# A norm's output turned by VectorE and DRAM instead of TensorE, ahead of the mixers of a two-layer trunk

## The chip, the core and the metric

The kernel runs on one core of a Trainium2 chip. The time is device microseconds of one execution; the median of several runs counts, and a separate execution is profiled. Engines are named as in the profile: PE is TensorE (PEld its weight loads), DVE is VectorE, ACT is ScalarE, POOL is GpSimd, SP is SyncE. PSUM is the memory that PE writes its results to, SBUF the memory that holds tiles of 128 partitions, and DRAM lies outside the core. A DMA is issued by SP, ACT or POOL and lands some microseconds later.

## What is computed

Two layers on a sequence of 256 rows of 1024 numbers. Each layer is a half-step SwiGLU feed-forward (FFN) and a norm, then three mixers that read the same normalised stream, another norm, and another FFN and norm:

```python
def hybrid_layer(x, mem_n, ...):
    h = layer_norm(DEEPNORM_ALPHA * x + 0.5 * swiglu(x, ffn1_w_gu, ffn1_w_down), ln_g[0], ln_b[0])
    (dn_q, dn_k, dn_v, dn_b, dn_a, dn_z, sw_q, sw_k, sw_v, xa_q, gates) = jnp.split(h @ w_in, split_idx, axis=-1)
    o_dn = deltanet_branch(dn_q, dn_k, dn_v, dn_b, dn_a, dn_z, ...)
    o_sw = sliding_window_attention(sw_q, sw_k, sw_v, swa_sinks)
    o_xa = memory_cross_attention(xa_q, mem_n, w_mem_kv)
    branches = jnp.stack([o_dn, o_sw, o_xa], axis=2)
    gates = jax.nn.sigmoid(gates.reshape(B_, S_, N_BRANCH, D))
    merged = jnp.sum(gates * jnp.einsum('bsnc,ncd->bsnd', branches, w_branch), axis=2)
    h = layer_norm(DEEPNORM_ALPHA * h + merged @ w_out, ln_g[1], ln_b[1])
    return layer_norm(DEEPNORM_ALPHA * h + 0.5 * swiglu(h, ffn2_w_gu, ffn2_w_down), ln_g[2], ln_b[2])
```

The change is at the first of these norms: its result h must be laid out with the 1024 channels on the partitions before `h @ w_in` can be computed. `memory_cross_attention` also needs keys and values of the 256 memory rows, `mem_n @ w_mem_kv`, which do not depend on h.

## The kernel before

All weights come as one stream (`wst`) in the order of their use. `unit` loads a piece of [128, 1024] (512 KB) by SP into a tile `raw`; `split` makes two tiles of it, `hi` by a cast on ACT (`whi`) and the remainder `lo` by a subtraction on DVE (`wlo`). Every product of two split operands is three matmuls (`mm3`): hi by hi, hi by lo, lo by hi. There are five buffers for each of whi and wlo and four for raw, so a unit's split waits until PE has used up the unit five ahead of it, and a load waits for the split four ahead.

The 256 rows are two blocks of 128 (tb 0 and 1). The residual stream lies in the tiles h0 and h1, rows on the partitions. The input of a projection lies turned in `hT`, channels on the partitions, split into hi and lo as well.

The place of the change, in each layer, is the end of the first FFN (`Ffn.rest`) and `memory_kv`:
- the down projection ends with the second row block, in two halves of 256 columns (tiles `at`), while the first block is already in the norm;
- `Post` adds the result to the residual and calls `layernorm` for each block (statistics L277 and L280, the root L284 on ACT, the scaling L291 and L296 on DVE in halves of 512 columns). After each half, `fin` turns it: for block 0 it leaves a closure that is called between the matmuls of block 1, for block 1 it turns at once;
- `to_T` turns four squares of 128 x 128 by PE transposes (L137) into one PSUM tile `sm`, and `split` casts it to hT's hi on ACT and subtracts for lo on DVE (L125);
- `memory_kv` projects the memory: the keys first (four weight units, tiles `acc<-w`), then the values (four units, tiles `acc<-whi,w`), which are copied from PSUM to `mv_` on ACT (L521). The splits of the value units are held behind the end of the norm (`behind=post.end`) in the order of their engines;
- `mixers` starts with a projection of hT in columns of 324 (tiles `acc<-whi,hT`), row block 0 before row block 1 in each unit. It writes four PSUM tiles `acc`; there are four buffers, and the last two of them are freed by the two value copies.

A scheduler orders each engine's instructions by priority; `tc.issue_after` keeps an instruction behind another one. From `mixers` on, PE's instructions keep their program order. Each engine runs its queue in order: an instruction that waits holds up all behind it.

The FFN already turns its hidden activations in another way (`Ffn.out`): DVE turns 32 x 32 squares inside a tile (L356), POOL stores the tile to DRAM in four DMAs that each take one quarter of the partitions (L362), and one DMA reads it back (L363), so that the squares come to lie on the right partitions. A channel order that differs from the natural one is made up for in the order of the weight's rows on the host.

In `inverses`, inside the mixers, POOL clears the tiles Y and X64 (L849, L850). They lie in buffers that the memory's turned rows leave, so the clears wait for PE to be done with those.

Of the kernel before, what the change touches and what calls it, by code (L numbers as in the profile page):

```python
# [17 lines left out]
P = 128  # L18
D = 1024
S = 256  # L20
# [3 lines left out]
KD = D // P  # L24
# [14 lines left out]
def tile_trunk(ctx, tc, x, xT, mem, memT_, wst, lnp, memln, cvw, rows, cst, out):  # L39
    nc = tc.nc  # L40
# [6 lines left out]
    p2 = ctx.enter_context(tc.tile_pool(name="p2", bufs=2))  # L47
# [4 lines left out]
    pd = ctx.enter_context(tc.tile_pool(name="pd", bufs=2, space=bass.MemoryType.DRAM))  # L52
# [71 lines left out]
    def split(hi, lo, src):  # L124
        return nc.scalar.copy(hi, src).ins, nc.vector.tensor_tensor(lo, src, hi.bitcast(F32), op=ALU.subtract).ins  # L125
# [183 lines left out]
    class Ffn:  # L309
        def __init__(self, before=None):  # L310
            self.units = []
            for q in range(KD // 2):
                if before:
                    before(q)
                self.units.append(unit(cuts=2 if before and q == 0 else 1, parts=2 if before and q in (1, 2) else 1))
            self.hu, self.bank, self.due = {}, {}, []
# [77 lines left out]

    class Post:

        def __init__(self, g_ap, b_ap, last=False):
            self.aps, self.last, self.hT = (g_ap, b_ap), last, None

        def early(self, bank):  # L400

# [6 lines left out]
        def __call__(self, tb, outs):  # L408
            if tb == 0:
                self.gb = gb(*self.aps)  # L410
                self.hT = None if self.last else new_hT()
            y = hres[tb]

            def put(q):
                return self.hT[0][:, q * 4:q * 4 + 4, :], self.hT[1][:, q * 4:q * 4 + 4, :]

            def src(j, c):
                nc.vector.scalar_tensor_tensor(y[:, c], outs[tb][j], 0.5 / ALPHA, y[:, c], op0=ALU.mult, op1=ALU.add)  # L418

            turns = []  # L420

            def fin(c):
                if self.last:

                    cc = slice(c * 512, (c + 1) * 512) if not tb else slice(*((0, 512), (512, 768), (768, 1024))[c])
                    (nc.scalar if c == 2 else nc.sync).dma_start(out[tb * P:(tb + 1) * P, cc], y[:, cc])
                elif tb == 0:

                    turns.append(lambda: to_T(put, tb, y, c))
                else:  # L430
                    to_T(put, tb, y, c)

            self.end = layernorm(y, *self.gb, 1, src, fin, [o.shape[-1] for o in outs[tb]], (512, 256, 256) if self.last and tb else (512, 512))
            return turns

    def begin(nxt, hT):
# [72 lines left out]
            return {8: lambda: again(0), 12: lambda: once(0), 14: lambda: again(1), 18: lambda: once(1)}  # L509
        return {4: vecs, 6: lambda: sums(0), 8: rows_, 11: halves_, 12: lambda: quarter(0), 14: lambda: quarter(1), 16: lambda: quarter(2), 18: lambda: quarter(3)}  # L510

    def memory_kv(mT, behind):
        mx = (lambda k: mT[k // 4][:, k % 4, :], lambda k: mT[2 + k // 4][:, k % 4, :])
        mkT = (T(pu, [P, 4, S], "u10", F32R), T(pu, [P, 4, S], "u7", F32R))
        for i, b in enumerate(projB(mx, 4, 2)):
            split(*(t[:, 2 * i:2 * i + 2, :] for t in mkT), b)
        mv_ = T(pu, [P, 2, 512], "u11")
        outs = [[acc()] for _ in range(2)]
        projA(mx, 512, 2, KD, outs, behind=behind, held=range(4))
        for tb in range(2):  # L520
            nc.scalar.copy(mv_[:, tb, :], outs[tb][0])  # L521
        return mkT, mv_

    def mixers(l, hT, mkT, mv_, post):
        xt = acc_of(hT)
        pinned[0] = True

# [128 lines left out]
        t = col("spt")  # L656
# [164 lines left out]
        def inverses():  # L821
# [21 lines left out]
            for j in range(15):  # L843
# [2 lines left out]
                nc.gpsimd.tensor_tensor(y16[:, :, j + 1:16], y16[:, :, j + 1:16], pr16[:, :, 0:n], op=ALU.add)  # L846
            nc.gpsimd.tensor_tensor(Y32.rearrange("p c h (d i) -> p (c h) d i", d=2), y16.unsqueeze(2).to_broadcast([P, 8, 2, 16]),
                                    cs[:, C_BD:C_BD + 32].rearrange("p (d i) -> p d i", d=2).unsqueeze(1).to_broadcast([P, 8, 2, 16]), op=ALU.mult)
            nc.gpsimd.memset(Y, 0.0)  # L849
            nc.gpsimd.memset(X64[qd[0], :, :, 32:64], 0.0)  # L850

        W = T(pu, [P, 1024], "w0")
        X64, X32, Y32 = (W[:, a:b].rearrange("p (c h i) -> p c h i", c=2, h=4) for a, b in ((0, 512), (512, 768), (768, 1024)))
# [277 lines left out]
    for l in range(NL):  # L1131
        mT = []
        mid = memory_T(mT, l)
        if l == 0:

            mid[2] = lambda: load(cs, cst)
            more = {4: lambda *a: xres(0), 6: lambda *a: xres(1), 8: lambda *a: small()}
        post = Post(lnp[l, 0, 0], lnp[l, 0, 1])
        f1.rest(hT, 4, [((pu, "u0"), (pu, "u1")), ((pu, "u2"), (pu, "u3"))], post, mid, ends, {} if l else more)
        kv = memory_kv(mT, post.end)  # L1140
        if l == 0:
            nc.scalar.activation(nea, rw[:, :, 8:12], AF.Exp)
            nc.vector.tensor_scalar(nea, nea, -1.0, None, ALU.mult)
        post2 = Post(lnp[l, 1, 0], lnp[l, 1, 1])
        mixers(l, post.hT, *kv, post2)
        f2 = Ffn()
        begin(f2, post2.hT)
        last = l == NL - 1
        post = Post(lnp[l, 2, 0], lnp[l, 2, 1], last)
        f2.rest(post2.hT, 6, [((pu, a), (pu, b)) for a, b in (("u0", "u1"), ("u2", "u3"), ("u4", "u5"), ("u6", "u13"))], post, behind=post2.end)  # L1150
        ends = post.end
        if not last:
            f1, hT = Ffn(), post.hT
            begin(f1, hT)
# [9 lines left out]
def _stream(i):  # L1164
    parts = []
    for l in range(NL):
# [6 lines left out]
        mk = i["w_mem_kv"][l]  # L1173
        parts.append(_kcols(mk[:, :512], 2))
        parts.append(_kcols(mk[:, 512:], 2))
        w = i["w_in"][l]
        parts.append(_kcols(np.concatenate([w[:, 1536:2056], w[:, 2696:2824]], 1), 1))
        for s in (512, 0, 1024, 2824):
            parts.extend(_kcols(w[:, c:c + 256], 4) for c in (s, s + 256))
# [62 lines left out]
```

## Time and profile before

| what | value |
|---|---|
| median of 3 runs | 1271.19 us (1271.11 to 1272.05) |
| the profiled execution: its time, its span | 1271.84 us, 1270.1 us |
| granted PE clock over the span | 0.999 |
| busy time of PE, DVE, ACT, POOL | 1258.1, 871.3, 661.5, 221.0 us |
| moved over the span | 263.56 MB, 208 GB/s |
| the norm's turn in layer 0: first and last group of transposes start | 186.64 and 195.03 us |
| the mixers' first projection starts (layer 0, layer 1) | 211.43 and 839.93 us |

A row of a timeline gives the start and the length in us, the engine, the line, the operation, output and inputs and the count; in brackets the idle time before it and what ended it. Neighbouring instructions on PE overlap, so PE's stream is read by the starts. In a row that groups instructions, behind the bar stand the busy time in us, the mean of one in ns, and the idle time before. For DMAs the last number is the median time in us from issue to landing.

### The profile page before, as it was taken

How to read it: one execution, taken by the hardware profiler on the slowest of the kernel's cores; microseconds unless marked ns; L12 is line 12 of the kernel's file. 1: busy time of each engine (PE TensorE's matmuls, PEld its weight loads, DVE VectorE, ACT ScalarE, POOL GpSimd, SP SyncE). 2: the span in 40 equal slices, each digit the busy share in tenths (PEclk: the TensorE clock that was granted, in tenths of full speed). 3: DMA queues.
4: the chain of work that ended last, by engine and by line, in shares of the span. 5: the costliest groups of instructions: out<-in, count | busy, mean ns of one | idle time of the engine just before them, and what ended most of it. 6: DMA issues, size and time to landing. Idle time of an engine off the chain costs nothing.

```text
span 1270.1 us, 18774 instructions
## 1 busy us (share of the span) xinstructions
PE 1258.1 (99%) x6916; PEld 1070.9 (84%) x6916; DVE 871.3 (69%) x1284; ACT 661.5 (52%) x982; POOL 221.0 (17%) x395
## 2 busy tenths in 40 slices
PE   9999999999999999999999999999999999999997
PEld 7888889999878888888888888899987788888886
DVE  6678576886667776665666665759776588766565
ACT  6456444655664544454454554455646654454441
POOL 1233000002331102221012220000023401122100
PEclk9999999999999999999999999999999999999999
DMA  8988765655554648787668887566554456578771
GB/s 293 322 265 286 249 210 160 205 179 137 164 151 150 240 139 258 243 242 220 215 208 246 256 255 216 178 185 212 162 158 133 134 189 226 174 248 243 240 231 74
DMA packets 78795, 263.56 MB, mean 208 GB/s; under 512 B 12528, under 2 KB 13968, under 8 KB 78704
## 3 DMA queue, kind: packets, MB, share of 16 engines
q1 hardware_dynamic: 66320, 232.40, 56.5%
q0 software_dynamic: 12240, 29.84, 8.7%
q8 instruction: 54, 0.88, 0.3%
q14 instruction: 37, 0.30, 0.1%
q10 hardware_dynamic: 144, 0.13, 0.0%
HBM read 247.48 MB, written 14.85 MB: 207 GB/s over the span
## 4 chain that ended last, share of the span: by engine, by line
PE 94%; DVE 3%; DMA 2%; ACT 1%; issue 1%; SPq 0%; DVEq 0%; ACTq 0%
PE acc L134 83%; PE at L134 3%; PE sm L134 3%; DMA raw<-in_wst_dram 2%; PE sm L137 1%; DVE wlo L125 1%; PE acc L335 1%; PE acc L332 1%; PE at L137 1%; PE acc L333 1%; ACT whi L125 1%; DVE h L291 0%; DVE h L296 0%; DVE h L418 0%; DVE bnst L277 0%
## 5 line engine op out<-in xcount | busy, mean ns | idle before, releaser
L125 DVE TENSOR_TENSOR wlo<-raw,whi 128x1024 fp32r<-128x1024 f32 (+2 forms) x405 | 487.1, 1210 | 277.0 <-ACT whi L125 275.0
L125 ACT CAST whi<-raw 128x1024 fp32r<-128x1024 f32 (+2 forms) x405 | 413.7, 1029 | 403.5 <-PE acc L134 314.8
L134 PE MATMUL acc<-whi,hT 128*128 128x512 f32 (+1 forms) x1824 | 563.1, 386 | 0.0
L134 PEld LDWEIGHTS acc<-whi,hT 128*128 128x128 f32 x1824 | 340.5, 188 | 68.9 <-issue 1.6
L134 PE MATMUL acc<-wlo,hT 128*128 128x512 f32 (+1 forms) x912 | 350.5, 384 | 0.1
L134 PE MATMUL acc<-whi,u 128*128 128x512 f32 x812 | 259.6, 392 | 0.0
L134 PEld LDWEIGHTS acc<-wlo,hT 128*128 128x128 f32 x912 | 171.6, 188 | 33.4 <-DVE wlo L125 0.9
L134 PEld LDWEIGHTS acc<-whi,u 128*128 128x128 f32 x812 | 152.3, 188 | 32.0 <-DVE u L125 0.5
L134 PE MATMUL acc<-wlo,u 128*128 128x512 f32 x406 | 158.2, 390 | 0.0
L362 POOL DMA_DIRECT2D tr<-t x176 | 96.0, 552 | 306.4 <-DVE t L356 299.4
L134 PE MATMUL acc<-hT,whi 128*128 128x256 f32 x672 | 121.8, 284 | 0.0
L134 PEld LDWEIGHTS acc<-hT,whi 128*128 128x128 f32 x672 | 104.7, 192 | 0.0
L134 PE MATMUL acc<-hT,wlo 128*128 128x256 f32 x336 | 95.1, 283 | 0.0
L134 PEld LDWEIGHTS acc<-wlo,u 128*128 128x128 f32 x406 | 76.3, 188 | 15.5
L134 PEld LDWEIGHTS acc<-hT,wlo 128*128 128x128 f32 x336 | 64.4, 192 | 0.0
L363 POOL DMA_DIRECT2D pt<-tr x44 | 25.0, 568 | 197.3 <-DMA tr<-t 151.6
L353 ACT ACTIVATE t<-acc 128x256 f32<-128x256 f32 x88 | 33.3, 379 | 37.1 <-PE acc L134 36.9
L134 PE MATMUL acc<-u,u 128*128 128x512 f32 x186 | 46.4, 394 | 0.0
L354 DVE TENSOR_TENSOR t<-t,acc 128x256 f32<-128x256 f32 x88 | 36.6, 417 | 8.1 <-ACT t L353 3.9
L134 PEld LDWEIGHTS acc<-u,u 128*128 128x128 f32 x186 | 34.6, 188 | 7.5
L553 DVE SCALAR_TENSOR_TENSOR t<-acc,cw,t 128x255 f32<-128x255 f32 (+2 forms) x72 | 34.5, 479 | 1.1
L125 DVE TENSOR_TENSOR u<-pt,u 128x512 fp32r<-128x512 f32 x44 | 28.9, 657 | 8.1 <-ACT u L125 8.1
(245 smaller groups left out, 1165.0 us busy)
## 6 DMA issues: line engine op xcount, KB each, us to landing
raw<-in_wst_dram SPq DMA_DIRECT2D x409, 512.0 KB, 4.4
tr<-t POOLq DMA_DIRECT2D x176, 64.0 KB, 3.9
pt<-tr POOLq DMA_DIRECT2D x44, 256.0 KB, 5.1
raw<-in_wst_dram SPq DMA_DIRECT2D x16, 324.0 KB, 3.0
gB<-in_lnp_dram SPq DMA_DIRECT2D x6, 512.0 KB, 6.7
bB<-in_lnp_dram SPq DMA_DIRECT2D x6, 512.0 KB, 7.0
w<-dr POOLq DMA_DIRECT2D x4, 512.0 KB, 12.6
t<-in_xT_dram SPq DMA_DIRECT2D x4, 256.0 KB, 5.4
```

The source lines that it names most:

```text
L125: return nc.scalar.copy(hi, src).ins, nc.vector.tensor_tensor(lo, src, hi.bitcast(F32), op=ALU.subtract).ins
L134: return pe(nc.tensor.matmul(*a, **k))
L137: return pe(nc.tensor.transpose(*a))
L332: nc.tensor.matmul(ps, hT[0][:, k, ts], hi[:, c], start=k == 0, stop=False)
L333: nc.tensor.matmul(ps, hT[0][:, k, ts], lo[:, c], start=False, stop=False)
L335: nc.tensor.matmul(ps, hT[1][:, k, ts], hi[:, c], start=False, stop=k == KD - 1)
L353: act = nc.scalar.activation(t[:, :, tb, :], g, AF.Silu).ins
L354: ins = nc.vector.tensor_tensor(t[:, :, tb, :], t[:, :, tb, :], u, op=ALU.mult).ins
L362: nc.gpsimd.dma_start(d[:, :, q].rearrange("b c x -> c b x"), z[32 * q:32 * q + 32].rearrange("c (b x) -> c b x", b=4))
L363: back = nc.gpsimd.dma_start(y, d.rearrange("b c q x -> (b c) (q x)")).ins
L553: nc.vector.scalar_tensor_tensor(yc[:, j, d:], b[:, j, :S - d], w[:, t:t + 1], yc[:, j, d:], op0=ALU.mult, op1=ALU.add)
```

## The change

The norm ahead of the mixers (and only this one of the three in a layer) is turned without PE. `fin` calls `leave` for each half: DVE turns its 32 x 32 squares into a tile z ("pp", L406 of the changed kernel). After a block's second half POOL stores z to a DRAM tile "tn" in four DMAs of 128 KB, in runs of 1 KB (L410). Behind the last store of block 1 POOL issues four reads, two for each block, of 256 KB in runs of 512 B (L417), into tiles "pt". `land` splits what has come back into hT: for block 0 behind the split of the keys in `memory_kv`, for block 1 ahead of the value copies. What the value units' splits are held behind is now the last DVE transpose. The two clears on POOL are held behind the last read. The rows of w_in are reordered on the host to match the new channel order. 16 PE transposes per layer, their four casts and four subtractions from PSUM go.

```diff
--- before.py
+++ after.py
@@ -394,8 +394,33 @@
 
     class Post:
 
-        def __init__(self, g_ap, b_ap, last=False):
+        def __init__(self, g_ap, b_ap, last=False, bounce=False):
             self.aps, self.last, self.hT = (g_ap, b_ap), last, None
+            self.bounce, self.backs = bounce, {}
+
+        def leave(self, tb, y, c):
+
+            if not c:
+                self.z = T(p2, [P, D], "pp")
+            cc = slice(c * 512, (c + 1) * 512)
+            ins = nc.vector.transpose(self.z[:, cc], y[:, cc]).ins
+            if c:
+                d = T(pd, [4, 32, 4, S], "tn")
+                for q in range(4):
+                    out_ = nc.gpsimd.dma_start(d[:, :, q].rearrange("b c x -> c b x"), self.z[32 * q:32 * q + 32].rearrange("c (b x) -> c b x", b=4)).ins
+                self.backs[tb] = d
+            if tb and c:
+                with tc.issue_after(out_):
+                    for t, d in self.backs.items():
+                        back = self.backs[t] = T(p2, [P, 2, 512], "pt")
+                        for i in range(2):
+                            self.read = nc.gpsimd.dma_start(back[:, i].rearrange("p (q x) -> p q x", q=4), d[:, :, :, i * P:i * P + P].rearrange("b c q x -> (b c) q x")).ins
+            return ins
+
+        def land(self, tb, c):
+            ts = slice(tb * P, (tb + 1) * P)
+            hi, lo = (self.hT[n][:, c * 4:c * 4 + 4, ts].rearrange("p k (q s) -> p q k s", q=4) for n in range(2))
+            return split(hi, lo, self.backs[tb][:, c].rearrange("p (q k s) -> p q k s", q=4, k=4))
 
         def early(self, bank):
 
@@ -424,6 +449,8 @@
 
                     cc = slice(c * 512, (c + 1) * 512) if not tb else slice(*((0, 512), (512, 768), (768, 1024))[c])
                     (nc.scalar if c == 2 else nc.sync).dma_start(out[tb * P:(tb + 1) * P, cc], y[:, cc])
+                elif self.bounce:
+                    self.left = self.leave(tb, y, c)
                 elif tb == 0:
 
                     turns.append(lambda: to_T(put, tb, y, c))
@@ -431,6 +458,8 @@
                     to_T(put, tb, y, c)
 
             self.end = layernorm(y, *self.gb, 1, src, fin, [o.shape[-1] for o in outs[tb]], (512, 256, 256) if self.last and tb else (512, 512))
+            if self.bounce:
+                self.end = self.left
             return turns
 
     def begin(nxt, hT):
@@ -509,19 +538,25 @@
             return {8: lambda: again(0), 12: lambda: once(0), 14: lambda: again(1), 18: lambda: once(1)}
         return {4: vecs, 6: lambda: sums(0), 8: rows_, 11: halves_, 12: lambda: quarter(0), 14: lambda: quarter(1), 16: lambda: quarter(2), 18: lambda: quarter(3)}
 
-    def memory_kv(mT, behind):
+    def memory_kv(mT, post):
+        behind = post.end
         mx = (lambda k: mT[k // 4][:, k % 4, :], lambda k: mT[2 + k // 4][:, k % 4, :])
         mkT = (T(pu, [P, 4, S], "u10", F32R), T(pu, [P, 4, S], "u7", F32R))
         for i, b in enumerate(projB(mx, 4, 2)):
-            split(*(t[:, 2 * i:2 * i + 2, :] for t in mkT), b)
+            ends = split(*(t[:, 2 * i:2 * i + 2, :] for t in mkT), b)
+        with tc.issue_after(ends[0]), tc.issue_after(ends[1]):
+            for c in range(2):
+                post.land(0, c)
         mv_ = T(pu, [P, 2, 512], "u11")
         outs = [[acc()] for _ in range(2)]
         projA(mx, 512, 2, KD, outs, behind=behind, held=range(4))
+        for c in range(2):
+            post.land(1, c)
         for tb in range(2):
             nc.scalar.copy(mv_[:, tb, :], outs[tb][0])
         return mkT, mv_
 
-    def mixers(l, hT, mkT, mv_, post):
+    def mixers(l, hT, mkT, mv_, post0, post):
         xt = acc_of(hT)
         pinned[0] = True
 
@@ -846,8 +881,9 @@
                 nc.gpsimd.tensor_tensor(y16[:, :, j + 1:16], y16[:, :, j + 1:16], pr16[:, :, 0:n], op=ALU.add)
             nc.gpsimd.tensor_tensor(Y32.rearrange("p c h (d i) -> p (c h) d i", d=2), y16.unsqueeze(2).to_broadcast([P, 8, 2, 16]),
                                     cs[:, C_BD:C_BD + 32].rearrange("p (d i) -> p d i", d=2).unsqueeze(1).to_broadcast([P, 8, 2, 16]), op=ALU.mult)
-            nc.gpsimd.memset(Y, 0.0)
-            nc.gpsimd.memset(X64[qd[0], :, :, 32:64], 0.0)
+            with tc.issue_after(post0.read):
+                nc.gpsimd.memset(Y, 0.0)
+                nc.gpsimd.memset(X64[qd[0], :, :, 32:64], 0.0)
 
         W = T(pu, [P, 1024], "w0")
         X64, X32, Y32 = (W[:, a:b].rearrange("p (c h i) -> p c h i", c=2, h=4) for a, b in ((0, 512), (512, 768), (768, 1024)))
@@ -1135,14 +1171,14 @@
 
             mid[2] = lambda: load(cs, cst)
             more = {4: lambda *a: xres(0), 6: lambda *a: xres(1), 8: lambda *a: small()}
-        post = Post(lnp[l, 0, 0], lnp[l, 0, 1])
+        post = Post(lnp[l, 0, 0], lnp[l, 0, 1], bounce=True)
         f1.rest(hT, 4, [((pu, "u0"), (pu, "u1")), ((pu, "u2"), (pu, "u3"))], post, mid, ends, {} if l else more)
-        kv = memory_kv(mT, post.end)
+        kv = memory_kv(mT, post)
         if l == 0:
             nc.scalar.activation(nea, rw[:, :, 8:12], AF.Exp)
             nc.vector.tensor_scalar(nea, nea, -1.0, None, ALU.mult)
         post2 = Post(lnp[l, 1, 0], lnp[l, 1, 1])
-        mixers(l, post.hT, *kv, post2)
+        mixers(l, post.hT, *kv, post, post2)
         f2 = Ffn()
         begin(f2, post2.hT)
         last = l == NL - 1
@@ -1173,7 +1209,7 @@
         mk = i["w_mem_kv"][l]
         parts.append(_kcols(mk[:, :512], 2))
         parts.append(_kcols(mk[:, 512:], 2))
-        w = i["w_in"][l]
+        w = i["w_in"][l].reshape(4, KD, 32, -1).transpose(1, 0, 2, 3).reshape(D, -1)
         parts.append(_kcols(np.concatenate([w[:, 1536:2056], w[:, 2696:2824]], 1), 1))
         for s in (512, 0, 1024, 2824):
             parts.extend(_kcols(w[:, c:c + 256], 4) for c in (s, s + 256))
```

DVE, layer 0, from the scaling of row block 0 (h0) to the aggregate of row block 1's statistics; wlo is the weight remainder of the last key unit, sm the turned squares in PSUM, at the end of the down projection. Before:

```order
L296 SCALAR_TENSOR_TENSOR h0_221<-h0_221,rstd_313_1610,bB_309_1599 128x512 x2
L418 SCALAR_TENSOR_TENSOR h1_222<-at_237_1211,h1_222 128x256
L125 TENSOR_TENSOR wlo_338_1802<-raw_336_1800,whi_337_1801 128x1024
L277 BN_STATS bnst_317_1671<-h1_222 128x6
L125 TENSOR_TENSOR hT_310_1602<-sm_315_1645,hT_310_1602 128x4x128
L125 TENSOR_TENSOR hT_310_1602<-sm_316_1664,hT_310_1602 128x4x128
L418 SCALAR_TENSOR_TENSOR h1_222<-at_238_1212,h1_222 128x256
L277 BN_STATS bnst_317_1671<-h1_222 128x6
L280 BN_AGGR bnmv_318_1679<-bnst_317_1671 128x2
```

Now:

```order
L296 SCALAR_TENSOR_TENSOR h0_221<-h0_221,rstd_313_1610,bB_309_1599 128x512 x2
L406 STREAM_TRANSPOSE pp_315_1620<-h0_221 128x512
L125 TENSOR_TENSOR wlo_340_1796<-raw_338_1794,whi_339_1795 128x1024
L406 STREAM_TRANSPOSE pp_315_1620<-h0_221 128x512
L443 SCALAR_TENSOR_TENSOR h1_222<-at_237_1211,h1_222 128x256
L443 SCALAR_TENSOR_TENSOR h1_222<-at_238_1212,h1_222 128x256
L277 BN_STATS bnst_317_1665<-h1_222 128x6 x2
L280 BN_AGGR bnmv_318_1673<-bnst_317_1665 128x2
```

Further on in the same queue of the changed kernel, from the scaling of row block 1 (h1) to the remainders of the four value units:

```order
L296 SCALAR_TENSOR_TENSOR h1_222<-h1_222,rstd_319_1675,bB_309_1599 128x512 x2
L406 STREAM_TRANSPOSE pp_321_1685<-h1_222 128x512 x2
L125 TENSOR_TENSOR wlo_346_1837<-raw_344_1835,whi_345_1836 128x1024
L125 TENSOR_TENSOR wlo_349_1855<-raw_347_1853,whi_348_1854 128x1024
L125 TENSOR_TENSOR wlo_352_1873<-raw_350_1871,whi_351_1872 128x1024
L125 TENSOR_TENSOR wlo_355_1891<-raw_353_1889,whi_354_1890 128x1024
```

Two transposes now stand where two subtractions from sm stood, and two more stand between the norm's end and the first value unit's wlo.

ACT, layer 0, from the split of the second half of the keys (u10) to the second value copy (u11 is mv_); whi of 128x648 are the first units of the mixers. Before:

```order
L125 CAST u10_323_1706<-acc_326_1709 128x512
L125 CAST whi_362_1936<-raw_361_1935 128x648
L125 CAST whi_365_1954<-raw_364_1953 128x648
L125 CAST whi_368_1972<-raw_367_1971 128x648
L521 COPY u11_339_1834<-acc_340_1835 128x512
L125 CAST whi_371_1990<-raw_370_1989 128x648
L521 COPY u11_339_1834<-acc_341_1836 128x512
```

Now:

```order
L125 CAST u10_325_1700<-acc_328_1703 128x512
L125 CAST whi_361_1920<-raw_360_1919 128x648
L125 CAST whi_364_1938<-raw_363_1937 128x648
L125 CAST whi_367_1956<-raw_366_1955 128x648
L125 CAST hT_310_1602<-pt_323_1694 128x4x4x32 x2
L125 CAST whi_370_1974<-raw_369_1973 128x648
L125 CAST hT_310_1602<-pt_324_1697 128x4x4x32 x2
L556 COPY u11_341_1832<-acc_342_1833 128x512
L125 CAST whi_373_1992<-raw_372_1991 128x648
L556 COPY u11_341_1832<-acc_343_1834 128x512
```

The casts of what has come back (hT<-pt, row block 0 and then 1) moved in front of the value copies.

POOL, layer 0, from the FFN's last read to the second clear, as it is now (before, the clears followed the first row directly):

```order
L363 DMA pt_231_1200<-tr_232_1201 128x512
L410 DMA tn_316_1624<-pp_315_1620 32x4x256 x4
L410 DMA tn_322_1689<-pp_321_1685 32x4x256 x4
L417 DMA pt_323_1694<-tn_316_1624 128x4x128 x2
L417 DMA pt_324_1697<-tn_322_1689 128x4x128 x2
L886 MEMSET w0_468_2586 32x8x32
L885 MEMSET w1_469_2587 128x1024
```

Eight stores and four reads moved in between, the reads of both blocks behind the stores of both.

## The prediction

> **What bounds the kernel now.** I read the page first (span, busy time, the chain that ended last), then the timeline of PE around the transposes, then the timelines of DVE, ACT and POOL at the same place. From the page:
>
> ```profile
> span 1270.1 us, 18774 instructions
> PE 1258.1 (99%) x6916; PEld 1070.9 (84%) x6916; DVE 871.3 (69%) x1284; ACT 661.5 (52%) x982; POOL 221.0 (17%) x395
> PE acc L134 83%; PE at L134 3%; PE sm L134 3%; DMA raw<-in_wst_dram 2%; PE sm L137 1%; DVE wlo L125 1%; PE acc L335 1%; PE acc L332 1%; PE at L137 1%; PE acc L333 1%; ACT whi L125 1%; DVE h L291 0%; DVE h L296 0%; DVE h L418 0%; DVE bnst L277 0%
> ```
>
> PE is the bound: busy 99%, and the chain is nearly all matmuls, with the transposes (L137) standing in it. So whatever leaves PE's stream shortens the span by its place in that stream, as long as nothing arrives late in its stead. The place itself, layer 0, in PE's timeline (start, length, instruction):
>
> ```profile
> 186.47 0.28 PE L134 MATMUL at<-whi,u 128*128 128x256 f32 x1
> 186.64 0.66 PE L137 MATMUL sm<-cs,h 128*128 128x128 f32 x4
> 187.05 0.36 PE L134 MATMUL acc<-w,whi 128*128 128x256 f32 x1
> 187.30 0.66 PE L137 MATMUL sm<-cs,h 128*128 128x128 f32 x4
> ...
> 187.91 0.28 PE L134 MATMUL acc<-w,wlo 128*128 128x256 f32 x1
> ...
> 193.72 0.40 PE L134 MATMUL acc<-w,whi 128*128 128x256 f32 x2
> ...
> 194.08 0.28 PE L134 MATMUL acc<-w,whi 128*128 128x256 f32 x1
> 194.32 0.63 PE L137 MATMUL sm<-cs,h 128*128 128x128 f32 x4
> 195.41 0.36 PE L134 MATMUL acc<-w,wlo 128*128 128x256 f32 x1
> ```
>
> **The change part by part: PE.** Sixteen transposes per layer leave the stream, four groups of four. Lengths overlap, so I count starts. Undisturbed, three matmuls of 256 columns take 0.36 us (193.72 to 194.08), 0.12 each. From 186.47 to 187.91 stand three such matmuls, 0.36 us, but 1.44 pass: the first two groups cost 1.08. From 194.08 to 195.41 stand two, 0.24 us, but 1.33 pass: the other two cost 1.09. Together 2.17 us in layer 0. Layer 1 shows the same place:
>
> ```profile
> 814.97 0.28 PE L134 MATMUL at<-whi,u 128*128 128x256 f32 x1
> 816.41 0.28 PE L134 MATMUL acc<-w,wlo 128*128 128x256 f32 x1
> ...
> 822.58 0.28 PE L134 MATMUL acc<-w,whi 128*128 128x256 f32 x1
> 823.91 0.36 PE L134 MATMUL acc<-w,wlo 128*128 128x256 f32 x1
> ```
>
> Again 1.44 and 1.33, so 2.17. Two layers: **4.34 us** off PE, if nothing takes their place. The order of PE's other rows is unchanged, and so is SP's.
>
> A mean duration would mislead here:
>
> ```profile
> L137 PE MATMUL sm<-cs,h 128*128 128x128 f32 x80 | 12.4, 279 | 0.5 <-DVE h L296 0.4
> ```
>
> Thirty-two times 0.279 us would be 8.9 us, but the next matmul starts 0.41 us after the first of four transposes (186.64 to 187.05), so a transpose takes a tenth of a microsecond of the stream. The Trainium skill ("TensorE: Matmul & The Clock Gate", Part 4: PE-mode transpose) gives about 275 ns for one in a kernel's context; as an estimate from that page 32 of them are 8.8 us and the sum would be 1263.0. The row's duration agrees with it, the spacing of the starts does not, and the spacing decides.
>
> **DVE.** What must come in time is read on the clock of before, with PE 2.17 us ahead of it behind the transposes.
>
> ```profile
> 185.85 1.40 DVE L296 SCALAR_TENSOR_TENSOR h<-h,rstd,bB 128x512 f32<-128x512 f32 x2
> 191.14 0.26 DVE L280 BATCH_NORM_AGGREGATE bnmv<-bnst 128x2 f32<-128x24 f32 x1
> 193.47 1.41 DVE L296 SCALAR_TENSOR_TENSOR h<-h,rstd,bB 128x512 f32<-128x512 f32 x2
> 194.80 3.49 DVE L125 TENSOR_TENSOR wlo<-raw,whi 128x1024 fp32r<-128x1024 f32 x3
> ...
> L356 DVE STREAM_TRANSPOSE t<-t 128x512 f32<-128x512 f32 x44 | 31.3, 711 | 1.3
> L277 DVE BATCH_NORM_STATS2 bnst<-h 128x6 f32<-128x256 f32 x24 | 9.8, 424 | 0.5
> L418 DVE SCALAR_TENSOR_TENSOR h<-at,h 128x256 f32<-128x256 f32 x12 | 5.0, 415 | 2.4 <-PE at L134 2.4
> ...
> 200.23 0.39 PE L134 MATMUL acc<-whi,w 128*128 128x512 f32 x1
> 211.43 0.31 PE L134 MATMUL acc<-whi,hT 128*128 128x324 f32 x1
> ```
>
> The first block's norm ends at 187.25. Up to the aggregate of the second block DVE now runs two transposes of 0.71, one weight remainder of 1.16 (3.49 for three), two L418 of 0.42 and two statistics of 0.42, and no longer the two hT remainders: 187.25 + 4.26 = 191.5, against 191.14. The rest of the norm is as long as before (191.14 to 194.88), so it ends at 195.25, its two transposes at 196.7. Behind them in DVE's queue stands the remainder of the first value unit, done at 197.9. PE starts on the values at 200.23 - 2.17 = 198.06 and needs that remainder with its second matmul. That fits by 0.2 us or more (the lengths are added whole, though instructions overlap a little); I cost it at nothing. Without that cover each microsecond of delay costs one per layer.
>
> **POOL and the DMAs.** Not shown by the trace of before: a store in runs of 1 KB (128 KB each) and a read in runs of 512 B (256 KB each). The nearest rows are the FFN's turning and that of the values among the mixers, on the same queue:
>
> ```profile
> 132.26 2.19 POOL L362 DMA_DIRECT2D tr<-t  x4 [5.25 <-DVE t L356]
> 138.40 0.57 POOL L363 DMA_DIRECT2D pt<-tr  x1 [3.94 <-DMA tr<-t]
> ...
> 355.93 4.44 POOL L605 DMA_DIRECT2D tv<-t  x8
> 364.04 0.56 POOL L610 DMA_DIRECT2D u<-tv  x1 [1.18 <-DMA tv<-t]
> ...
> pt<-tr POOLq DMA_DIRECT2D x44, 256.0 KB, 5.1
> w<-dr POOLq DMA_DIRECT2D x4, 512.0 KB, 12.6
> u<-tv POOLq DMA_DIRECT2D x4, 256.0 KB, 3.2
> ...
> 130.00:143.00 13.00, 13.00 (x59) 10.75 (x58) 8.01 (x9) 7.34 (x9) 2.76 (x5) 1.00 0.91 307
> 355.00:367.00 12.00, 12.00 (x121) 9.64 (x121) 6.32 (x9) 11.13 (x30) 6.39 (x13) 1.00 0.82 235
> 197.00:211.00 14.00, 14.00 (x76) 11.89 (x75) 8.06 (x11) 5.64 (x8) 0.30 (x1) 1.00 0.56 166
> ```
>
> The second block's four stores are issued from 196.8 on (0.1 for the handover) at 0.55 each (2.19 for four); the last starts at 198.5. A last store was waited for until 4.5 us after its issue in the FFN (133.9 to 138.4) and 4.2 in the mixers (359.8 to 364.0): landed at 202.7. Then come this block's two reads; those of the first block went out before them. A read lands after 3.2 us (values) to 5.1 us (FFN), so the second block's first half is back between 205.9 and 207.8. The last three rows are stretches (share of the DMA engines busy and GB/s at the end): the new transfers run where the DMA engines are busy 0.56, below both neighbours, so I take the values' 3.2 and **205.9**, and leave the rest to the shorter runs.
>
> **ACT, where a late read would show.** The two casts of the second block now stand ahead of both value copies (L521), and PE's last two banks of the first projection are those that the copies set free.
>
> ```profile
> 210.23 0.59 ACT L521 COPY u<-acc 128x512 f32<-128x512 f32 x1 [0.67 <-PE acc L134]
> 211.63 0.73 ACT L125 CAST whi<-raw 128x648 fp32r<-128x648 f32 x1 [0.81 <-PE acc L134]
> 212.27 0.58 ACT L521 COPY u<-acc 128x512 f32<-128x512 f32 x1
> ```
>
> The first projection now starts at 211.43 - 2.17 = 209.26. The weight cast between the two copies waits for PE and can't start before 209.46 (211.63 - 2.17). Ahead of it ACT needs the two casts, of the copies' size and so some 0.6 each, and a copy of 0.59: a first half that is back by **207.7** delays nothing. With 205.9 there is 1.8 us to spare; every microsecond past 207.7 is one lost per layer. The clears on POOL stand behind the reads, and their first reader is the inversion inside the mixers, a later stage: nothing. The new row order of w_in is made on the host.
>
> **The sum.** Off PE 4.34, added to the path nothing: the profiled execution took 1271.84 us (span 1270.1 and 1.7 around it), so 1267.5. It lies 0.65 above the median of the runs, so I predict 1271.2 - 4.3 = **1266.9**, a gain of 0.34%.
>
> **The rivals.**
> 1. *The read is late and eats part of the gain.* With the FFN's 4.5 and 5.1 the half is back at 198.5 + 9.6 = 208.1, 0.4 past the limit: 0.8 us lost, 1267.7. At the gain's end it would be 2.17 past, 1271.2. For it: runs of 512 B and stores of twice the size, unseen here. Against: the freer DMA engines. 17%.
> 2. *The read is so late that the kernel gets slower.* Place: ACT's wait for the second block's read, with the value copies behind it. It decides from 207.7 + 2.17 = 209.9, that is from 7.2 us for the read after stores landed at 202.7. The one slow read of this queue (w<-dr, 12.6) would bring 215.3: 7.6 lost per layer, 15.2 - 4.3 = 10.9 slower, 1282.1. Against: it is 512 KB, broadcast, in pairs. 5%.
> 3. *DVE holds up POOL's issues.* If each issue waited for the DVE instruction in progress (1.16), four stores and a read would be 5.8 us later, the half back at 211.7, 4.0 past the limit: 8.0 - 4.3 slower, 1274.9. Against it stands the spread of one issue over all 176 stores, beside a DVE that is busy 69%:
>
> ```profile
> L362 POOL DMA_DIRECT2D tr<-t x176: 548/550/709, 21.4 to 1210.3; - x176
> ```
>
> The Trainium skill ("SBUF — State Buffer", SBUF: two separate sides) warns that GpSimd can't write descriptors while VectorE runs in a two-port mode, 620 ns becoming some 3100; the estimate from that page, 2.5 us more for each of five issues, would be 1271.2 - 4.3 + 2 x 10.7 = 1288.3. The row, at most 709, disagrees for the instructions that run here. 2%.
> 4. *The held value weights are late on DVE.* If DVE's norm is 1 us longer than counted, 0.8 per layer is lost: 1268.5. 5%.
> 5. *Transposes cost PE their whole record*: 1271.2 - 8.9 = 1262.3. 1%.
> 6. *The gain goes back later*, since PE waits for weights that it reaches 2.17 us sooner: 1271.2. Against: PE is busy 99% behind this place. 3%.
>
> **How the numbers follow.** My forecast, no new wait, has 67% with its own range 1266.0 to 1268.0 (the runs spread by 0.9). About 0.2%, 2.5 us, is what a measurement of this kernel can tell from no change; faster by more ends at 1268.7. Faster: 67 + 1 + 4 of the fourth + 10 of the first = 82%. Within: 7 of the first, 1, 3 and 1 of the second = 12%. Slower: 6%. Range 1265.9 to 1270.5: it takes in the forecast, the fourth and most of the first (its 0.8 and up to 1.8 us of waiting per layer), and leaves out some 15%.
>
> **What would show it.** PE: no sm<-cs,h rows at these two places, "acc<-w" at the spacing of 0.12, and the first hT matmul 2.17 us nearer to the last "at" matmul. POOL: stores of 0.55, the second block's reads issued about 4.2 us after its last store, landing in 3 to 5. ACT: no idle time put down to the second block's read, the second copy directly behind its weight cast. I am wrong if PE idles before an hT matmul, or before the first value matmul that needs wlo.

## The result and the profile after

The change made the kernel slower: 1273.96 us median (22 runs, 1271.10 to 1278.81) against 1271.32 before on the same chip (22 runs, 1269.87 to 1276.62), a ratio of **1.0023 (95% interval 1.0016 to 1.0030)**. The forecast was 1266.9, the range 1265.9 to 1270.5. The profiled execution of the changed kernel took 1272.81 us. From its page:

```profile
span 1270.9 us, 18754 instructions
PE 1254.2 (99%) x6884; PEld 1067.2 (84%) x6884; DVE 874.7 (69%) x1292; ACT 661.4 (52%) x982; POOL 235.9 (19%) x419
L134 PE MATMUL acc<-whi,hT 128*128 128x512 f32 (+1 forms) x1824 | 563.4, 386 | 3.8 <-ACT u L556 3.8
```

PE runs 32 instructions fewer and is busy 3.9 us less, and yet the span is 0.8 longer. The last row holds the new thing: 3.8 us in which matmuls waited for the value copies (L556; L521 before), where the same row of before has no idle time. Set one by one beside their partners of before (the 32 transposes left out), the matmuls of this execution start earlier or later by the following steps (negative is earlier):

| place | layer 0 | layer 1 |
|---|---|---|
| the norm's turn | -2.2 | -2.2 |
| the mixers' first projection | +0.9 | +3.35 |
| the second norm | +1.1 | +0.9 |
| elsewhere | within 0.3 | -0.9 near 970 us |

So the saving came as counted, and layer 1's first projection alone gave back more than that layer had saved. POOL's timeline of the changed kernel, both layers (start, length, what, and in brackets the idle time before it and what ended it):

```profile
196.14 2.18 POOL L410 DMA_DIRECT2D tn<-pp  x4 [4.10 <-DVE pp L406]
198.31 1.51 POOL L417 DMA_DIRECT2D pt<-tn  x2
202.80 1.49 POOL L417 DMA_DIRECT2D pt<-tn  x2 [2.97 <-ACT whi L125]
...
824.42 1.09 POOL L410 DMA_DIRECT2D tn<-pp  x2 [4.11 <-DVE pp L406]
827.89 1.09 POOL L410 DMA_DIRECT2D tn<-pp  x2 [2.37 <-issue]
828.98 1.52 POOL L417 DMA_DIRECT2D pt<-tn  x2
833.25 1.49 POOL L417 DMA_DIRECT2D pt<-tn  x2 [2.75 <-ACT whi L125]
```

In layer 0 block 1's reads start at 202.80, as predicted (202.7). (The releaser named there is the last by the profile, but ACT has nothing to do with a store; what the reads wait for is the stores' landing.) In layer 1 a pause of 2.37 us stands between the second and the third store, with "issue" as its cause: POOL waits for nothing that the profile shows. How long the reads take, over all eight (a group's issue time in ns, then issue to landing in us):

```profile
L417 POOL DMA_DIRECT2D pt<-tn x8: 749/752/768, 198.3 to 834.0; - x8
DMA to landing us min/median/max: 5.0/6.0/6.7
```

The prediction took 3.2. ACT, in layer 0 and in layer 1, at the casts of block 1 and the value copies behind them:

```profile
209.25 0.62 ACT L125 CAST hT<-pt 128x512 fp32r<-128x512 f32 x1 [0.27 <-DMA pt<-tn]
209.78 0.58 ACT L556 COPY u<-acc 128x512 f32<-128x512 f32 x1
...
839.22 0.62 ACT L125 CAST hT<-pt 128x512 fp32r<-128x512 f32 x1 [2.16 <-DMA pt<-tn]
840.00 0.62 ACT L125 CAST hT<-pt 128x512 fp32r<-128x512 f32 x1 [0.17 <-DMA pt<-tn]
840.53 0.58 ACT L556 COPY u<-acc 128x512 f32<-128x512 f32 x1
```

And PE, at the same place of layer 1:

```profile
838.12 0.31 PE L134 MATMUL acc<-whi,hT 128*128 128x324 f32 x1
841.16 0.42 PE L134 MATMUL acc<-whi,hT 128*128 128x324 f32 x1 [2.73 <-ACT u L556]
...
842.28 0.42 PE L134 MATMUL acc<-whi,hT 128*128 128x324 f32 x1 [0.41 <-ACT u L556]
```

This is the place that the second rival named: the read lands, the casts run, the copies behind them free the two PSUM banks late. Some of the wait belongs to the order on ACT and not to the read: the first cast of block 1 ended at 839.84, PE went on at 841.16 behind the first copy and stood another 0.41 us for the second. No run puts the copies ahead of the casts, so how the wait divides between the two isn't shown. Why the read is late is in the DMA engines' share (next to last column; GB/s last), in the stretch where block 1's stores and all reads travel. Before:

```profile
200.00:208.00 8.00, 8.00 (x38) 6.49 (x37) 4.23 (x7) 3.00 (x5) 0.30 (x1) 1.00 0.54 160
828.00:836.00 8.00, 8.00 (x40) 6.58 (x39) 4.56 (x7) 3.27 (x5) 0.30 (x1) 1.00 0.64 188
```

After:

```profile
200.00:208.00 8.00, 8.00 (x36) 6.44 (x35) 4.41 (x7) 3.42 (x6) 1.81 (x3) 1.00 1.03 353
828.00:836.00 8.00, 8.00 (x36) 6.40 (x35) 4.74 (x7) 3.02 (x5) 4.31 (x7) 1.00 1.01 336
```

The engines are full for eight microseconds. Half of the stores and all reads, 1.5 MB, over 8 us are some 190 GB/s; on top of the 160 that ran there before, that is about the 353. The total fits better than its parts: of the packets that started from 200 to 208 us, those of POOL's queue make 160 GB/s and the weight loads 192; from 828 to 836 us they make 98 and 238, so the weight loads themselves moved more there than before.

### The profile page after: what moved, and what is told of

The parts are those of the page before. It is cut to its first block, busy times and chain, and to the rows that moved or that the text cites. A ratio compares the mean times of both kernels' runs of the same rounds, so it can differ in the third digit from the quotient of the medians.

```text
span 1270.9 us, 18754 instructions
## 1 busy us (share of the span) xinstructions
PE 1254.2 (99%) x6884; PEld 1067.2 (84%) x6884; DVE 874.7 (69%) x1292; ACT 661.4 (52%) x982; POOL 235.9 (19%) x419
## 4 chain that ended last, share of the span: by engine, by line
PE 88%; DMA 4%; DVE 3%; issue 2%; POOL 2%; ACT 1%; DVEq 0%; POOLq 0%; ACTq 0%
PE acc L134 79%; PE at L134 3%; PE sm L134 3%; DMA raw<-in_wst_dram 2%; DVE wlo L125 2%; DMA w<-dr 1%; PE sm L137 1%; PE acc L335 1%; PE acc L332 1%; PE acc L333 1%; ACT whi L125 1%; PE at L137 1%; POOL t L880 1%; DMA pt<-tn 0%; POOL l L871 0%
## 5 line engine op out<-in xcount | busy, mean ns | idle before, releaser
L1074 POOL TENSOR_TENSOR u<-u,gt 128x512 f32<-128x512 f32 x16 | 20.8, 1298 | 78.2 <-DVE gt L1072 74.2
```

The lines of the kernel that those rows point to most:

```text
L1074: nc.gpsimd.tensor_tensor(mg[tb][:, js], mg[tb][:, js], gt[tb][:, js], op=ALU.add)
```

## The experiments

Each is the changed kernel with one edit, unless said otherwise. Times are medians; ratios are to the kernel before (1272.36 us for the first four, 1272.06 for the next four, 1271.92 in one execution for the last three), measured on the same chip.

**Without the trip, and with the trip unread.** In the first, stores and reads are left out; in the second they run, but nobody reads what comes back. Both split the tile z in place of the tile that came back, so the channels don't lie where the weights expect them, and all other work stays (without the trip, the two clears wait for the last transpose):

```diff
-            return split(hi, lo, self.backs[tb][:, c].rearrange("p (q k s) -> p q k s", q=4, k=4))
+            return split(hi, lo, self.zs[tb][:, c * 512:(c + 1) * 512].rearrange("p (q k s) -> p q k s", q=4, k=4))
```

> Leaves out the stores and the reads: hT is split straight from the tile that DVE's transposes wrote, so channel blocks don't come to their partitions; all other work stays, the transposes on PE gone. Theory A (the second block's reads land about 6 us after their issue, the value copies stand behind their casts on ACT, and PE waits for both) and theory B (the new transfers slow the weight loads): the 4.34 us off PE stay whole in both, 1271.3 - 4.3 = 1267.0, ratio 0.9966, no wait before an hT matmul beyond the 0.25 us of before. Theory C (taking the transposes out of PE's stream does not shorten it, or DVE's two longer places cost it): 1270 or more.

> Keeps all stores and reads of the changed kernel, but splits hT from the transposed tile, as in the run without the trip; so the transfers run and nobody waits for what they bring. A alone: as without the trip, 1267.0. B: ACT still waits for raw units of the mixers (2.93, 1.66 and 1.30 us before the first three in layer 0 of the changed kernel), and PE for the copies behind them; 0.5 to 1.5 us per layer stay lost, 1268 to 1270.

Without the trip 1267.89 us, ratio 0.9967 (0.9954 to 0.9979); with the trip unread 1268.02, ratio 0.9970 (0.9957 to 0.9983). So the 4.3 us of transposes are real, and some 4 MB of extra traffic costs nothing as long as nothing waits for it: the weights have room. The loss is that the read is waited for, and what follows from that wait.

**Longer runs.** Each read takes two quarters of the features, in runs of 2 KB instead of 512 B, and needs only the stores of its two quarters (`land` takes its half out of both reads):

```diff
-self.read = nc.gpsimd.dma_start(back[:, i].rearrange("p (q x) -> p q x", q=4), d[:, :, :, i * P:i * P + P].rearrange("b c q x -> (b c) q x")).ins
+self.read = nc.gpsimd.dma_start(back[:, i], d[:, :, 2 * i:2 * i + 2].rearrange("b c q x -> (b c) (q x)")).ins
...
```

> The same reads, number and bytes, but cut by quarters of partitions and not by halves of channels: runs of 2 KB in place of 512 B. If the short runs make the reads slow (A1): issue 0.57 in place of 0.75, landing 3.2 to 5 in place of 6.0, the second block back 1.5 to 3 us sooner, 1268 to 1270.5. If the load on the DMA engines does (A2): landing stays at 5.5 to 6.5 and the time at 1273 to 1274.

1270.03 us, ratio 0.9987 (0.9977 to 0.9997). The issue fell from 0.75 to 0.56 us, but the reads still landed after 6.1 (5.4 to 6.7): short runs were not what made them slow. So the landing came out as the second theory (A2) had it, the time as the first (A1). By the trace, the gain came from earlier issues (200.5 and 202.5 in layer 0) and because the pause of 2.37 us no longer stood among layer 1's stores.

**More of block 0 first.** Three weight units of the projection run on block 0 before block 1 is needed, instead of one:

```diff
-        projA(xt, MOD, 1, KD, outs, 3)
+        projA(xt, MOD, 1, KD, outs, 3, (), 3)
```

> The first projection of the mixers takes three weight units with row block 0 before row block 1 has its first turn (three times 0.885 us of work where there was one), so PE first needs the second block and the value copies 1.77 us later. A and B: up to 1.77 us per layer come back, 1270 to 1271.5. If PE's wait lay elsewhere (C): 1274.

1270.04 us, ratio 0.9983 (0.9971 to 0.9996). PE still waited 1.6 us for the value copies in layer 1.

**Both together.**

> The changed kernel with two edits together: the reads cut by quarters of the features, so that each run of data is 2 KB, and three weight units of the mixers' projection on block 0 ahead of block 1's (two before). If what is lost is only that the two halves of the trip come too late for TensorE, the two add up: the first alone left 1.1 us of TensorE's waits at the projection, and a third unit of block 0's products is worth about 2 us there, so no wait of TensorE above 0.5 us in either layer and a time of 1267.6 to 1269.0 us, ratio to before 0.9965 to 0.9980. If something else holds part of the loss (the transfers' load on the weights, a later give-back), it stays at 0.998 to 0.999, where each edit alone was.

**1267.60 us, ratio 0.9964 (0.9950 to 0.9977): faster than both kernels**, and level with the kernel that makes no trip at all. (Its expectation counts two units of block 0 ahead in the changed kernel; there is one.) PE's three longest waits by releaser (total, times, longest):

```profile
PE sm L1154 <- DVE pp L1151: 1.5, 1, 1.5
PE acc L134 <- ACT whi L125: 0.9, 1, 0.9
PE sm L137 <- DVE h L296: 0.6, 2, 0.4
```

The 1.5 us at the kernel's start stand in the kernel before as well. The value copies (L556) are gone from the list, although the reads land no sooner (6.5 median). The wait of 0.9 lies at 9.6 us, in the first FFN; at the mixers' projection PE is busy throughout in both layers.

**Is it the load, or what such a read costs?** Three runs. First, block 0's reads directly behind block 0's stores:

```diff
+                with tc.issue_after(self.read) if tb else nullcontext():
...
-            if tb and c:
                 with tc.issue_after(out_):
-                    for t, d in self.backs.items():
+                    for t, d in ((tb, d),):
```

> The changed kernel, but block 0's two reads stand right behind block 0's four stores on GpSimd's queue, ahead of block 1's stores. They are then issued near 195 to 197 us in layer 0, where the transfer engines' share was 0.04 to 0.33, and block 1's reads have their stretch with half a megabyte less in it. Theory 'load' (a read lands late because stores, reads and weight loads fill the engines from 200 to 208 us): block 0's reads land in 2.5 to 4.5 us after issue, block 1's in 4 to 5.5. Rival 'a read costs that' (512 runs of 512 bytes each from the software queue need 6 us whatever else moves): all land in 5.5 to 6.5. The time hangs on block 1's stores, which leave some 1.3 us later, against a shorter landing: 1271.5 to 1274.

The first one, issued at 195.55 before the engines fill, landed after 3.5 us; the one behind it, at 196.3, after 5.7. The window holds the first of them alone:

```profile
L416 POOL DMA_DIRECT2D pt<-tn x1: 766/766/766, 195.5 to 195.5; - x1
DMA to landing us min/median/max: 3.5/3.5/3.5
```

The later ones took 4.2 to 5.8, so neither theory got its band whole. Block 1's stores left 0.9 us later and took longer to land, and the time was 1274.20, just past the expected range, ratio 1.0014 (1.0002 to 1.0025). Second, the reads on ACT's queue (`nc.scalar` for `nc.gpsimd`):

> The changed kernel with its reads issued by ScalarE's own queue instead of GpSimd's; the stores stay on GpSimd's. ScalarE waits in its order for the stores, so its casts move. Theory 'load': the reads still land in 4.5 to 6.5 us, as they share the same full engines. Rival 'the software queue is slow': they land in about 3 us, like the read of 256 KB that took 3.2 us before. GpSimd's queue has 2048 runs fewer in each layer, so that by the count of runs (below, the moved pause) the pause of 2.4 us falls elsewhere. Time between 1268 and 1274 us: it hangs on where ScalarE is held.

From a queue that POOL has no part in the reads took 3.9 to 8.0 us, 5.4 at the median. None landed in the 3 us of the rival (3.9 at the least): the queue is not the cause. ACT itself was held longer: PE waited 3.6 us in one piece in each layer, 1277.24 us, ratio 1.0040 (1.0027 to 1.0052), over the range that was expected. Third, the weight loads of the mixers held until the trip is over:

```diff
+        seen = T(pd, [P, 2], "seen")
+        mark.append(nc.sync.dma_start(seen, post0.backs[1][:, 1, 0:2]).ins)
         projA(xt, MOD, 1, KD, outs, 3)
...
+                with tc.issue_after(mark[0]) if mark else nullcontext():
                     nc.sync.dma_start(raw[:, c], src[:, c])
```

> The changed kernel with one small store on the hardware queue that the weight loads use: it waits for block 1's last read, and the mixers' weight loads stand behind it in that queue. So the trip has the transfer engines to itself, and the mixers start some 8 to 12 us later in each layer, for want of weights: 1285 to 1305 us, which says nothing of the change. What counts is from issue to landing of the reads of 256 KB. Theory 'load': they land in 2.5 to 4.5 us (3.5 was the earliest-issued one's time with block 0's reads ahead, 3.2 that of the kernel's other read of the same size). Rival 'a read of 512-byte runs costs that': 5.5 to 6.5 us as before.

One execution, 1281.56 us, less than the 1285 that was expected at least. Its reads, all eight:

```profile
L418 POOL DMA_DIRECT2D pt<-tn x8: 747/752/766, 198.3 to 837.0; - x8
...
DMA to landing us min/median/max: 3.4/3.5/3.6
```

The same transfer from the same queue takes 3.5 instead of 6.0 once the weight loads are out of its way, and the stores land sooner too: block 1's reads could start at 201.22 instead of 202.80. **Load it is**: the weight loads and the trip together. Whether a read waits for the bytes ahead of it or for the number of transfers, no run separates.

**The pause of 2.37 us.** The kernel before has such pauses too, where they do no harm (POOL's timeline):

```profile
546.59 2.18 POOL L362 DMA_DIRECT2D tr<-t  x4 [6.75 <-issue]
...
1116.73 0.57 POOL L363 DMA_DIRECT2D pt<-tr  x1 [7.11 <-issue]
```

They come after a like count of runs on POOL's queue. So 16 small stores were added in an idle stretch ahead of layer 1:

```diff
+        if not l:
+            pad = T(pd, [16, P, 1], "pad", bufs=1)
+            with tc.issue_after(f2.last[2]):
+                for n in range(16):
+                    nc.gpsimd.dma_start(pad[n], zero)
```

> The changed kernel with 16 extra stores of one number from each of 128 partitions on GpSimd's queue, in layer 0's last idle stretch (near 586 to 595 us), where nothing waits for them. Theory 'count': GpSimd pauses 2.2 to 7 us whenever its queue has issued some 13,500 to 14,800 runs (counting 128 a transfer, 512 for the reads with runs of 512 bytes: 14,720 and 13,312 in the kernel before, 14,848 and 13,568 in the changed one). The 16 stores then bring the second pause forward by 16 transfers, from between layer 1's stores at 827.9 us to the product's stores near 747 us, where the kernel before has such a pause without loss; layer 1's reads leave 2.4 us earlier and the loss at layer 1's mixers falls from 3.35 us to about 1, the time to 1271.0 to 1272.3 us (2 to 2.5 us under the changed kernel). Rival 'place' (the pause comes from the stores themselves or from load at that place): the pause stays at layer 1's third store, and the time at that of the changed kernel.

The pause moved, the time did not follow: 1285.35 us, ratio 1.0103 (1.0089 to 1.0118). POOL's timeline of it:

```profile
764.96 2.18 POOL L362 DMA_DIRECT2D tr<-t  x4 [6.47 <-DVE w L125]
...
839.12 2.17 POOL L410 DMA_DIRECT2D tn<-pp  x4 [4.11 <-DVE pp L406]
841.28 1.51 POOL L417 DMA_DIRECT2D pt<-tn  x2
```

Layer 1's four stores now leave in one piece. The stores at 764.96, which are the sixteenth transfer before the third of those stores, leave 2.9 us after their data is there (DVE's last transpose ends at 762.09); in the changed kernel the same ones left 0.3 after. (The row names w, a tile that the same stores did not wait for in the changed kernel.) So the pause goes by count, not by place. PE's wait at layer 1's projection fell from 3.1 to 1.7. By the matmuls' starts layer 1 lost 2.0 us there instead of 3.35. But the 16 stores of 512 bytes cost some 15 us by themselves at the FFN's end. DMA share and GB/s while they ran:

```profile
585.00:590.00 5.00, 5.00 (x23) 4.14 (x23) 2.01 (x3) 2.09 (x2) 2.02 (x4) 1.00 1.36 183
590.00:595.00 5.00, 5.00 (x23) 4.13 (x22) 1.26 (x3) 1.67 (x2) 1.30 (x3) 1.00 0.75 48
```

They landed 10.3 to 14.6 us after issue, the weight loads beside them 9.3 to 15.0 us after theirs (4.1 to 5.4 in the changed kernel), and PE ran dry. That was in no theory.

**Why the median lies over the profiled execution.** Two more profiled executions of the changed kernel as it is:

> The changed kernel as it is, for a second profiled execution. The first one took 1272.81 us, 1.2 under the median of its 22 runs, at a mean granted clock of 0.998 where most of the 22 show 0.995 to 0.997; TensorE waited 2.73 us at layer 1's mixers in it with no drop of the clock. Theory 'clock': in most executions that wait is followed by a stretch of about 3.4 us at half clock, as in the kernel with block 0's reads ahead (0.59 from 840 to 844 us, after a wait of 2.5 us) and the one with ScalarE's reads (0.77 and 0.80 from 212 to 220 us, after 3.6 us); a profiled execution of 1273.5 us or more then shows a granted clock under 0.9 within 8 us of the wait, worth 1 to 2 us. Rival 'other': such an execution shows full clock there, and the time lies in longer waits.

> As again1, a third profiled execution of the changed kernel: if it takes 1273.5 us or more, a granted clock under 0.9 in the 8 us after layer 1's wait (theory 'clock'), or full clock and longer waits (rival 'other').

1273.00 and 1274.81 us. Granted clock (third from the end) in the 8 us around the end of layer 1's wait, in the first of the two:

```profile
840.00:844.00 4.00, 2.95 (x13) 2.69 (x14) 2.26 (x3) 2.44 (x5) 0.00 (x0) 0.81 0.23 56
844.00:848.00 4.00, 4.00 (x22) 4.00 (x22) 0.93 (x2) 1.14 (x2) 0.00 (x0) 0.76 0.57 207
```

In the execution profiled first:

```profile
840.00:844.00 4.00, 2.44 (x14) 2.17 (x15) 2.30 (x4) 2.96 (x5) 0.00 (x0) 1.00 0.13 36
844.00:848.00 4.00, 4.00 (x29) 4.00 (x28) 2.12 (x3) 1.47 (x2) 0.00 (x0) 1.00 0.70 240
```

The second of the two shows 0.84 and 0.73. Theory "clock" holds, in an execution that it did not claim (1273.00) as well. The missing clock is (0.19 + 0.24) x 4 = 1.72 us, which is 3.44 us at half clock; the second gives (0.16 + 0.27) x 4, the same. The waits were as long in all three (2.73, 3.0 and 2.9 us), so a wait near 3 us brings the drop in some executions and not in others. The record of the 22 runs fits: the three with a mean clock of 0.998 or more took 1271.1 to 1272.8 us, the other 19, at 0.994 to 0.997, took 1271.6 to 1278.8; one drop of 1.72 us is 0.0014 of the span. That every one of the slower runs lost its clock at this place isn't shown, since only three executions were profiled.

## Why the prediction was wrong

Three terms of it failed: the landing of the read was sized too short, and the pause on POOL in layer 1 and TensorE's clock after the wait were put at nothing. Term by term:

- **PE's saving, 2.17 us per layer: right.** The alignment shows 2.2 in each layer, and the kernel without the trip is 4.5 us faster than before. Rival 5 (whole durations, 8.9) falls, and with it the 275 ns of the Trainium skill ("TensorE: Matmul & The Clock Gate", Part 4: PE-mode transpose) as a price in the stream. The prediction's 1263.0 for that price starts from the profiled execution, 1271.84; from the median, as its other sums do, it would be 1262.4.
- **DVE: right.** The transposes ended at 195.84 (counted 196.7), the value weights were in time, no wait of PE stands there. Rival 4 fell.
- **POOL's issue and the stores: right in layer 0 by luck** (202.80 against 202.7). The last store left at 197.77, 0.7 sooner than counted, and block 1's first read followed it after 5.0 us instead of 4.2; the two errors cancel. Rival 3 fell: an issue took 552 to 557 ns beside a busy DVE.
- **The read's landing: the step that failed.** The prediction took the values' 3.2 us and not the FFN's 5.1, since "the new transfers run where the DMA engines are busy 0.56, below both neighbours". It took 5.0 for the first half and 5.7 for the second in layer 0, 5.9 and 6.0 in layer 1. The 0.56 was the mean of a window of 14 us of the kernel *before*: it lacked the trip's own 1.5 MB, and it averaged over a burst of weight loads (up to 0.82 from 200 to 202) and the quiet after it. With the trip's bytes added, 160 + 190 GB/s in 200 to 208, the rows would have shown full engines: the FFN's row of before moved 307 GB/s at a share of 0.91, which puts full near 340. Held weights bring the landing back to 3.5, so the price chosen was that of a road that isn't full (from 364.0 to 367.2 us, over the values' own read, the share was 0.76).
- **Which half decides.** The limit of 207.7 was set for the first half; it came at 207.8, on the limit. But the second half was issued 0.75 later and landed at 209.2, and its cast stands ahead of the copies as well. Layer 0 lost 0.9: rival 1.
- **Layer 1 was taken to be like layer 0.** The pause of 2.37 us among its stores, which the trace of before showed elsewhere (6.75 and 7.11 us, "issue"), put its reads past 209.9's counterpart: 3.35 us lost, rival 2's place and mechanism at a smaller size. The prediction put this pause at nothing without a word. The late landing alone would have left a gain: 0.9 us lost in layer 0 and 2.0 in layer 1 (the run with the moved pause) against 4.3 saved.
- **The sum.** Not in the prediction at all: the clock after a wait of 3 us. Without a drop of the clock: -4.3 + 0.9 + 3.4 + some 1.1 at layer 0's second norm = 1.1 slower (layer 1's +0.9 and -0.9 cancel); with one drop, up to 1.7 more, 2.8. The medians differ by 2.6. As for the 1.1, PE waits 1.0 to 1.7 at the transposes of that norm in the three profiles of the changed kernel and 1.0 in the kernel without the trip, against 0.4 before, but 0.4 with the trip unread and none with both edits. So it isn't simply that PE comes sooner (rival 6); its cause is open.

## What to carry to other kernels

Price a transfer by the bytes in flight in its own stretch, its own included: the stretch's GB/s before plus the new bytes over the stretch, against what the engines moved when full (here 336 to 353 GB/s over 8 us); a mean over a longer window hides the burst. When a result leaves the core and comes back, the gain lives or dies by slack: give the engine that is the bound other work (here two more units of block 0's products) and let each piece be waited for alone, before trying to make the transfer faster. Each of the two alone gave 1270.0 us, both together 1267.6. And look for the same step in every layer: a pause that comes by count falls on another place in each.

## What the runs showed of the hardware

- **TensorE's clock drops after a short wait.** The drops seen at the mixers cost 1.72 us of clock, as 3.44 us at half, or twice that (3.4 us in each layer with the weights held, after waits of 3.5 and 5.5); in the run with the small stores one cost three times as much (5.1 us, around a wait of 4.9). With block 0's reads ahead, after a wait of 2.5 us (0.08 of the 1.72 lie in the 4 us before this row):

```profile
840.00:844.00 4.00, 4.00 (x16) 3.78 (x17) 2.12 (x3) 1.35 (x2) 0.00 (x0) 0.59 0.44 159
```

  The Trainium skill ("TensorE: Matmul & The Clock Gate", Part 1: The HAM clock gate) tells of a free-running window of about 3.4 us and of half clock after an idle window. The length agrees with 3.44. That waits of 2.5 to 3.0 us already bring it, in some executions, is less than the idle window that the Trainium skill gives there; a window that need not be wholly idle would fit, but no run here tests it.
- **POOL pauses by count.** Counting 128 runs a transfer (512 for the reads of 512-byte runs), the pauses come after 14,720 and again 13,312 in the kernel before, after 14,848 and 13,568 in the changed one; 2.2 to 2.9 us each, what POOL waits for anyway (some 4.2 in the two rows of before) taken off. With the reads issued by ACT, POOL pauses after the same 115 and 219 transfers as in the kernel before, at 528.88 and 999.77 us instead of 546.59 and 1116.73. What it does in the pauses no view shows.
- **Tiny stores are not cheap.** Sixteen stores of one number from each of 128 partitions, 8 KB in all, kept the engines at shares of 0.75 to 1.36 for 10 us and more, and the weight loads beside them landed after 9.3 to 15.0 us instead of 4.1 to 5.4.
